# Column mean of an 8192 x 8192 matrix: which rows of the matrix each SBUF partition loads

## The chip, the cores and the metric

The kernel runs on one core of a Trainium2 chip. The metric is device time in microseconds (us) of one execution; the median of three runs of the kernel before is 627.79 us (627.75 to 627.97).

## The reference

The input `x` is a float32 matrix of 8192 x 8192, 256 MiB. The output is the mean of each column, 8192 numbers:

```python
def reference(x: np.ndarray) -> np.ndarray:
    return np.mean(x, axis=0)
```

Every input byte is needed once, and one addition is made per element.

## The kernel before, in words

Rows lie in memory one after the other, 32 KB each. A *slab* is 128 rows, one for each of the 128 SBUF partitions; there are 64 slabs. The first 62 are loaded as 31 *pairs*: a pair is 256 successive rows, 8 MB, and partition p takes rows 2p and 2p + 1 of the pair, which are 64 KB in one stretch. The helper `rows` (lines 58 to 60) forms this source. Three buffers `pairs[0..2]` of 128 x 16384 float32 are used in turn.

All loads are issued by SyncE, in order, on one DMA queue. `load` (line 77) issues the load of a pair, at line 83. Most loads take a whole pair. The first is cut after 2048 columns (`FIRST`), and the last three are cut between the two rows (`BY_ROW`). From pair 3 on, SyncE waits before a load until VectorE has added up the pair that the buffer held before (line 95, semaphore `read`). One load is carried out by sixteen DMA engines, each of which serves eight partitions.

VectorE does nearly all the adding, all at line 53. For each pair it waits until the data has landed (`take`, line 56, in the loop of line 99; by row at lines 105 and 107), adds the first rows to the running sum of the pair before, and then the second rows to that. Each of these is one instruction on 128 x 8192 elements. So one running sum per partition and column moves from buffer to buffer.

The last two slabs are loaded by themselves. The next to last, `slab`, comes in three loads (line 163), the last, `last`, in nine pieces of falling width (`PIECES`, line 166). TensorE sums over the partitions: it multiplies the running sum, the slab and the last slab by a matrix of ones, and accumulates in PSUM (`fold_wide` and `fold_narrow`, line 136), piece by piece as the last slab lands. VectorE adds the last quarter of `slab` itself. ScalarE and VectorE scale the totals by 1/8192 (lines 151 and 153), and SyncE stores them (lines 200 and 215).

The order of work on every engine is written out by hand, with semaphores; no planner rearranges it.

Of the kernel before, what the change touches and what calls it, by code (L numbers as in the profile page):

```python
# [21 lines left out]
def kernel(  # L22
# [5 lines left out]
    nc = tc.nc  # L28
    P = nc.NUM_PARTITIONS
    R, C = x.shape  # L30
    n_slabs = R // P
# [23 lines left out]
    def take(sem, n):  # L55
        nc.vector.wait_ge(sem, n).then_inc(sem, -n)  # L56

    def rows(k):
        src = x[2 * P * k : 2 * P * (k + 1), :]
        return src.rearrange("(p j) c -> p (j c)", j=2)  # L60

    def first_rows(b):
        ins = add(pairs[b][:, 0:C], pairs[b][:, 0:C], pairs[b - 1][:, 0:C])
# [13 lines left out]
    def load(k):  # L77
        b = k % 3
        cut = FIRST if k == 0 else C if k >= n_pairs - BY_ROW else 2 * C
        for lo, hi in ((0, cut), (cut, 2 * C)):  # L80
            if lo < hi:
                sem = second[b] if lo == C else landed[b]
                ins = nc.sync.dma_start(out=pairs[b][:, lo:hi], in_=rows(k)[:, lo:hi])
                yield ins.then_inc(sem, 16)
# [34 lines left out]
    def behind(ins, wait=False):  # L119
        kind = mybir.DependencyClass.Sync if wait else mybir.DependencyClass.NoSync  # L120
        info = mybir.DependencyInfo(kind, mybir.DependencyReason.DATA)
        tc.add_manual_dep(ins.ins, section.name, info, reason="the last pair's second rows")

    wide, lo = [], 0
# [31 lines left out]


    tail = pairs[n_pairs % 3]
    r = (n_slabs - 2) * P
    slab, last = tail[:, 0:C], tail[:, C : 2 * C]  # L160
    parts = [(lo, lo + w) for lo, w, _ in wide[:3]] + [(wide[3][0], C)]
    for lo, hi in ((0, C // 4), (C // 4, C // 2), (C // 2, C)):
        behind(nc.sync.dma_start(out=slab[:, lo:hi], in_=x[r : r + P, lo:hi]))  # L163
    lo = 0
    for w in PIECES:
        nc.sync.dma_start(out=last[:, lo : lo + w], in_=x[r + P : R, lo : lo + w])  # L166
        lo += w


# [3 lines left out]
    lo, hi = parts[3]  # L173
# [70 lines left out]
```

## Time and profile before

| | before |
|---|---|
| median of three runs | 627.79 us |
| profiled execution, its own time | 627.46 us |
| its span in the profile | 625.5 us |
| DMA engines, share of the span | 99.4% |
| read from HBM | 268.44 MB |
| mean rate over the span | 429 GB/s |
| VectorE busy | 533.6 us (85%) |
| one VectorE add, 128 x 8192 | 8.69 us |
| TensorE busy | 13.5 us (2%) |

The profile is of one execution. Its span goes from the first to the last instruction that the profiler records; the execution's own time is about 2 us longer. "Busy" is time in which an engine carries out an instruction of its own. For the DMA engines the share is the time that their packets took, in percent of sixteen engines' span. A wait is written as the engine and line that waited, an arrow, and what released it; a name like DVEq or SPq is the engine's own sequencer, in which a semaphore wait stands ahead of the work. DVE is VectorE, PE TensorE, ACT ScalarE, SP SyncE.

### The profile page before, as it was taken

Reading aid. Unit: us, or ns where it says so; the run is one execution under the profiler, and the core shown is the slowest. Engines: PE = TensorE matmul, PEld = TensorE weight load, DVE = VectorE, ACT = ScalarE, POOL = GpSimd, SP = SyncE. Lnnn points to the kernel's source line nnn. Section 1 sums busy time; section 2 is a strip of 40 time slices with the busy share of each in tenths; the row PEclk is TensorE's granted clock in tenths of the full one; section 3 lists DMA queues with packets and bytes.
Section 4 is the critical chain, followed back from the end, with each engine's and each line's share of the span. In section 5 each row is a group of like instructions: output and inputs, shape, how many; then the busy total and the mean of one; then the engine's idle time right before and its main releaser. Section 6 shows DMA issues by size and latency. Waiting matters only on the chain. (4 is left out here: it accounts for less than half of the span.)

```text
span 625.5 us, 520 instructions
## 1 busy us (share of the span) xinstructions
PE 13.5 (2%) x106; PEld 4.2 (1%) x106; DVE 533.6 (85%) x67; ACT 4.2 (1%) x7; POOL 0.3 (0%) x5
## 2 busy tenths in 40 slices
PE   0000000000000000000000000000000000000007
PEld 0000000000000000000000000000000000000002
DVE  0538988889888899888898888988889888899995
ACT  0000000000000000000000000000000000000001
POOL 0000000000000000000000000000000000000000
PEclk9999999999999999999999999999999999999999
DMA  9999999999999999999999999999999999999997
GB/s 404 400 469 402 469 402 469 402 469 402 469 402 465 407 423 448 402 469 402 469 402 469 402 469 402 469 402 469 402 461 411 440 432 419 423 432 436 436 429 312
DMA packets 6797, 268.49 MB, mean 429 GB/s; under 512 B 890, under 2 KB 1406, under 8 KB 1548
## 3 DMA queue, kind: packets, MB, share of 16 engines
q1 hardware_dynamic: 6796, 268.47, 99.4%
q8 instruction: 1, 0.02, 0.0%
HBM read 268.44 MB, written 0.03 MB: 429 GB/s over the span
## 5 line engine op out<-in xcount | busy, mean ns | idle before, releaser
L53 DVE TENSOR_TENSOR pair<-pair,pair 128x8192 f32<-128x8192 f32 (+1 forms) x31 | 263.1, 8486 | 60.9 <-DVEq L56 60.3
L53 DVE TENSOR_TENSOR pair<-pair 128x8192 f32<-128x8192 f32 (+1 forms) x34 | 269.7, 7938 | 23.8 <-DVEq L56 22.7
L136 PE MATMUL wide<-pair,ones 128*32 128x512 f32 (+1 forms) x88 | 12.0, 688 | 609.3 <-DVE pair L53 608.6
L136 PEld LDWEIGHTS wide<-pair,ones 128*32 128x32 f32 x88 | 3.2, 130 | 617.4 <-issue 614.1
L151 ACT ACT_TABLE_LOAD x1 | 1.3, 1283 | 602.9 <-ACTq L112 602.9
L153 DVE TENSOR_SCALAR row<-narrow 1x256 f32<-1x256 f32 x2 | 0.8, 415 | 4.8 <-PE narrow L136 4.8
L136 PE MATMUL narrow<-pair,ones 128*32 128x256 f32 (+2 forms) x18 | 2.0, 359 | 0.0
L151 ACT ACTIVATE rw<-wide 128x512 f32<-128x512 f32 x3 | 1.8, 597 | 15.6 <-PE wide L136 15.6
L136 PEld LDWEIGHTS narrow<-pair,ones 128*32 128x32 f32 x18 | 1.0, 109 | 0.9 <-DMA pair<-in_x_dram 0.5
L151 ACT ACTIVATE row<-narrow 1x256 f32<-1x256 f32 x2 | 0.8, 376 | 0.5 <-PE narrow L136 0.5
L151 ACT ACTIVATE r<-wide 128x256 f32<-128x256 f32 x1 | 0.4, 384 | 0.1
L92 POOL MEMSET ones<- 128x32 f32 x1 | 0.1, 124 | 0.3 <-POOLq L228 0.3
L228 POOL MEMSET const-bfloat16-1.0<- 128x1 bf16 x1 | 0.1, 101 | 0.0
L228 POOL MEMSET const-uint8-127<- 128x1 uint8 x1 | 0.1, 101 | 0.0
L228 POOL MEMSET const-float32-0.0<- 128x1 f32 x1 | 0.1, 98 | 0.2 <-issue 0.2
L228 POOL MEMSET const-float32-1.0<- 128x1 f32 x1 | 0.1, 98 | 0.0
## 6 DMA issues: line engine op xcount, KB each, us to landing
pair<-in_x_dram SPq DMA_DIRECT2D x6, 4096.0 KB, 25.5
pair<-in_x_dram SPq DMA_DIRECT2D x1, 7168.0 KB, 21.3
pair<-in_x_dram SPq DMA_DIRECT2D x6, 1024.0 KB, 8.7
pair<-in_x_dram SPq DMA_DIRECT2D x1, 2048.0 KB, 14.0
pair<-in_x_dram SPq DMA_DIRECT2D x1, 512.0 KB
pair<-in_x_dram SPq DMA_DIRECT2D x27, 29.7
pair<-in_x_dram SPq DMA_DIRECT2D x3, 128.0 KB, 15.5
pair<-in_x_dram SPq DMA_DIRECT2D x1, 80.0 KB, 9.9
```

Source lines behind the costliest of these rows:

```text
L53: return nc.vector.tensor_tensor(out=dst, in0=a, in1=b, op=ADD)
L92: tc.declare_fence(nc.gpsimd.memset(ones, 1.0).ins, group="ahead")
L136: nc.tensor.matmul(out=dst, lhsT=ones, rhs=src, skip_group_check=True, **flags)
L151: nc.scalar.mul(out=dst, in_=src, mul=inv_r)
L153: nc.vector.tensor_scalar(out=dst, in0=src, scalar1=inv_r, scalar2=None, op0=mybir.AluOpType.mult)
L228: nc = _bacc.Bacc("TRN2", target_bir_lowering=False, num_devices=1)
```

## The change

The 64 rows that a partition adds up are chosen differently. Partition p now holds rows 64p to 64p + 63. Load k takes from every partition's block its rows 2k and 2k + 1, again 64 KB in one stretch. The two last slabs are the rows 62 and 63 of every block. Between neighbouring partitions the source moves by 64 rows, 2 MB, in place of 64 KB (pairs) or 32 KB (slabs); between the first partitions of neighbouring DMA engines, by 16 MB in place of 512 KB. The mean is over all rows, so the result is the same up to the order of the additions.

```diff
+
+    by_part = x.rearrange("(p s) c -> p s c", s=n_slabs)
+
     def rows(k):
-        src = x[2 * P * k : 2 * P * (k + 1), :]
-        return src.rearrange("(p j) c -> p (j c)", j=2)
+        return by_part[:, 2 * k : 2 * k + 2, :].rearrange("p j c -> p (j c)")
...
     tail = pairs[n_pairs % 3]
-    r = (n_slabs - 2) * P
     slab, last = tail[:, 0:C], tail[:, C : 2 * C]
...
-        behind(nc.sync.dma_start(out=slab[:, lo:hi], in_=x[r : r + P, lo:hi]))
+        behind(nc.sync.dma_start(out=slab[:, lo:hi], in_=by_part[:, n_slabs - 2, lo:hi]))
     lo = 0
     for w in PIECES:
-        nc.sync.dma_start(out=last[:, lo : lo + w], in_=x[r + P : R, lo : lo + w])
+        nc.sync.dma_start(out=last[:, lo : lo + w], in_=by_part[:, n_slabs - 1, lo : lo + w])
         lo += w
```

## The prediction

> **What bounds the kernel now.** I read the page's busy shares first, then its DMA part, then a table of busy time and transfer rate by stretches, then the waits, and last the chain that set the end.
>
> ```profile
> span 625.5 us, 520 instructions
> PE 13.5 (2%) x106; PEld 4.2 (1%) x106; DVE 533.6 (85%) x67; ACT 4.2 (1%) x7; POOL 0.3 (0%) x5
> DMA packets 6797, 268.49 MB, mean 429 GB/s; under 512 B 890, under 2 KB 1406, under 8 KB 1548
> q1 hardware_dynamic: 6796, 268.47, 99.4%
> ```
>
> VectorE is busy for 85% of the span, but the sixteen DMA engines for 99.4%. They have no gap to fill: 99.4% of 625.5 us is 621.7 us, and all but a start of about 2 us and an end of about 2 us is transfer.
>
> The table by stretches gives busy time of each engine, granted clock, then the mean share of the DMA engines and their GB/s. Records are counted by whole transfers, so a share can read over 1; the quotient of the last two columns is the rate of a busy engine set.
>
> ```profile
> 0.00:2.00 2.00, 0.00 (x0) 0.00 (x0) 0.00 (x0) 0.00 (x0) 0.33 (x5) 1.00 0.33 49
> 3.00:4.00 1.00, 0.00 (x0) 0.00 (x0) 0.00 (x0) 0.00 (x0) 0.00 (x0) 1.00 1.02 434
> 20.00:120.00 100.00, 0.00 (x0) 0.00 (x0) 78.86 (x10) 0.00 (x0) 0.00 (x0) 1.00 1.00 431
> 120.00:220.00 100.00, 0.00 (x0) 0.00 (x0) 90.27 (x11) 0.00 (x0) 0.00 (x0) 1.00 1.00 432
> 320.00:420.00 100.00, 0.00 (x0) 0.00 (x0) 90.32 (x12) 0.00 (x0) 0.00 (x0) 1.00 0.99 430
> 420.00:520.00 100.00, 0.00 (x0) 0.00 (x0) 90.34 (x11) 0.00 (x0) 0.00 (x0) 1.00 1.02 440
> 610.00:615.00 5.00, 5.00 (x32) 1.39 (x28) 5.00 (x3) 0.00 (x0) 0.00 (x0) 1.00 0.98 416
> ```
>
> The quotient is 431, 432, 434 and 431 GB/s in the four long rows: it does not move. The single transfer records say the same more sharply: the 3,456 pieces of 64 KB (one piece is what one partition takes from one load) have a median of 2.418 us, the shortest is 2.415 and the longest 2.575; 65,536 bytes in 2.418 us on 16 engines is 433.7 GB/s. The 768 pieces of 32 KB all take 1.213 us. So today the engines run at a rate of their own and the memory never holds them up. Only the first row differs: 49 GB/s at a share of 0.33 is 148 GB/s while busy. Its sixteen first records, 8 KB each, took 0.68 to 1.16 us, 0.86 in the mean, where later pieces of 8 KB take 0.309.
>
> ```profile
> DVE pair L53 <- DVEq L56: 49.6, 26, 2.0
> SPq L83 <- DVEq L69: 557.8, 28, 48.0
> DMA 3%; PE 1%; SPq 0%; ACT 0%; issue 0%
> ```
>
> The first line is the waits between 60 and 560 us: before each pair of rows VectorE waits about 1.9 us for data. A pair needs 2 x 8.69 = 17.4 us of adding and 8 x 2.418 = 19.3 us of loading. The second line, SyncE waiting for VectorE to free a buffer, looks large and costs nothing: it waits with two loads queued ahead. The chain that ended last is made of the last slab's loads, then some 5 us of matmul, scaling and store. The kernel is its load stream: 620 us of data at 433 GB/s, and 7.5 us around it up to the profiled execution's own 627.46 us (its span is 625.5). That is 0.33 us, 0.05%, under the median of 627.79, so the sum below stands for either.
>
> **The change, part by part.** *Instructions.* The diff touches source addresses only. Loads, SyncE's issues (328 ns each at line 83), waits, adds, matmuls and stores stay in number and order: 0 us, and nothing is queued behind anything new. *Pieces.* Each load still takes 64 KB in one stretch per partition (8 to 56 KB where it is cut), and the row sums take part in a mean over all rows, so any distribution of rows serves. Per engine: 27 loads x 8 partitions = 216 pieces of 64 KB, 8 of 56 KB and 8 of 8 KB from load 0, 6 x 8 = 48 of 32 KB from the loads cut by row, 24 from the slab and 72 from the last slab: 376, of which 272 are of 32 KB or more. Same counts after: 0 us.
>
> *Places.* This is the only cost. Before, a pair is one block of 8 MB, and engines at 8 partitions each stand 512 KB apart; afterwards partitions are 64 x 32 KB = 2 MB apart and engines 16 MB. Whether the memory serves sixteen streams at such distances at 433 GB/s is not in the trace. From below: a gain can only come out of what the engines now lose to memory. That is 0.55 us at the first records and (2.4197 mean - 2.418) x 216 = 0.4 us, about 1 us together. From above: the row in which memory sets the time is the start, where a piece pays 0.86 - 0.31 = 0.55 us more; on all 376 pieces of an engine that is 207 us, so 835 us.
>
> Between 0 and 207 us I take a loss. For none speak two rows: the slab's pieces, whose partitions lie only 32 KB apart in place of 64, run at the same rate (its 16 KB pieces take 0.611 us, a quarter of 2.418 and 0.006), so halving a distance did nothing; and an engine's step from one load to the next, which jumps past the other engines' blocks, leaves no piece longer than 2.575 us. But both were seen at distances up to 8 MB inside one block, and all sixteen engines together covered every address of that block. After the change sixteen streams that are equally far have all address digits below 2 MB in common; a memory whose parts are chosen by these digits serves them by turns. The nearest row for an engine that waits for memory is the start, and of it I take the smallest extra, 0.68 - 0.31 = 0.37 us, since some of a first access comes once only. I charge it to the pieces of 32 KB or more: at the start the second piece of an engine took 0.31 to 0.46 us, so small pieces overlap each other. 272 x 0.37 = 101 us; 627.5 + 101 = 728.5 us, say **729**. A 64 KB piece then takes 2.79 us, the stream runs at 376 GB/s, and a pair takes 22.3 us. Nothing covers this, since the DMA engines have no idle time. VectorE is no bound at either rate; its wait grows from 1.9 to about 4.9 us per pair and takes nothing off.
>
> A rule speaks against the change. The Trainium skill, on the page "DMA: Bandwidth & Descriptors", section "Latency and other measured facts", reports copies between tensors in HBM with one row per partition: 207 GB/s in each direction at a pitch of 512 KiB, 164 at 2 MiB and 103 at 4 MiB, restored by a padding of 4 KiB. By the ratio 164/207 the 620 us become 783 and the kernel 790 us, an estimate from that page. No run here shows a pitch of 2 MB yet; the copies write to HBM too, which this stream doesn't.
>
> **The rivals.** *Nothing changes, 627.5 us (chance 0.23).* The memory has room for sixteen streams wherever they are. For it: the constant 2.418 us, the unmoved slab. Against it: both come from close places. It decides if 64 KB pieces stay at 2.42 us.
>
> *Full contention, around 835 us (0.24, from 765 up).* The streams meet at one part of memory throughout, and every piece, small ones too, pays what the first ones paid: 376 x 0.55 = 207 us. For it: engines with like addresses have nothing to drive them apart except their own delays. Against it: those delays do drive them apart, and a stream that has fallen behind by one part of memory no longer collides. It takes the place of the forecast from 0.5 us extra per large piece (136 us). About a third of it lies beyond 835. I give it as much as no change, since the rows show both what a first access costs and that close places cost nothing, and none lies at 2 MB. The Trainium skill's rule above, 790 us, would fall in this case; no trace so far bears on that.
>
> *A small loss, 629 to 663 us (0.09).* The pieces stretch no more than the longest seen: 2.575 - 2.418 = 0.157 us on 216 + 8 pieces is 35 us. That is what memory refusals already look like mid-run, rarely.
>
> *Faster (0.04).* The place is the start and the few stretched pieces: if the engines, far apart, no longer hinder one another there, the 1 us above is won, 626.5 us. It would have to be more than 1.26 us, 0.2%, to decide, and the rows hold no more; the chance stands for what they can't show. A faster stream in the middle is excluded as far as the rows reach: a piece that never varies isn't waiting for memory.
>
> **How the numbers follow.** The forecast, a sustained loss of 0.13 to 0.5 us per large piece, has a chance of 0.40, and its own range is 663 to 765 us. With 0.24, 0.23, 0.09 and 0.04 for the others that makes 1. Slower by over 0.2% (about 1.26 us, what a measurement of this kernel can tell from no change): 0.40 + 0.24 + 0.09 = 0.73. Within: 0.23. Faster: 0.04. The range must hold both no change and most of full contention, so it goes from 626.5 (the lower edge of no change) to 835; outside lie the faster case, 0.04, and some 0.08 above.
>
> **What would show it.** In the DMA part the share should stay near 99% while the mean falls from 429 to about 370 GB/s, with the same 6,800 packets. The 64 KB records should have a median near 2.8 us and a spread, where now there is none; the wait at line 56 should rise to about 5 us per pair; the adds should stay at 8.69 us. If the pieces stay at 2.42 us, the step from addresses to contention is wrong. If they stretch to 3 us or more, my price per piece was too low; if only the tail from 598 us on grows, it is the small pieces that pay, against my choice. Different packet counts would mean that the loads were cut otherwise, which I hold excluded.

## The result and the profile after

The change makes the kernel slower: median 663.83 us of eight runs (653.85 to 670.3) against 627.77 (627.43 to 627.97). The ratio is 1.0435, 95% interval 1.0421 to 1.045; it rests on the three shortest of the eight runs, because the other five, the profiled one among them, lie over 1.5% above the shortest, and the kernel before shows no such scatter. Two later sets of four gave 1.0559 (1.0516 to 1.0602) and 1.03 (1.0283 to 1.0317) on two different chips. So the medians of the sets lie 19 to 36 us above the kernel before, and the loss is not a fixed number. I had forecast 101.

The profiled execution after took 664.72 us. These lines of its page are the span, the GB/s in 40 equal slices, the packets and the load queue's share:

```profile
span 662.8 us, 520 instructions
GB/s 285 364 396 415 431 407 427 443 411 411 415 407 439 423 407 439 439 423 419 431 439 411 415 439 407 419 443 427 435 423 423 439 443 415 392 425 415 363 278 115
DMA packets 6797, 268.49 MB, mean 405 GB/s; under 512 B 890, under 2 KB 1406, under 8 KB 1548
q1 hardware_dynamic: 6796, 268.47, 98.3%
```

Instructions and packets are the same as before, and the DMA engines are still busy all the time. They do the same work at 405 instead of 429 GB/s. The slices show where: at 285 and 364 in the first two, 278 and 115 in the last two, and in between a little under the old rate. The table by stretches (columns as in the prediction: clock, DMA share and GB/s at the end of each line) says the same for the changed kernel in absolute time:

```profile
0.00:20.00 20.00, 0.00 (x0) 0.00 (x0) 0.00 (x0) 0.00 (x0) 0.33 (x5) 1.00 0.86 282
20.00:40.00 20.00, 0.00 (x0) 0.00 (x0) 8.69 (x1) 0.00 (x0) 0.00 (x0) 1.00 1.03 396
100.00:200.00 100.00, 0.00 (x0) 0.00 (x0) 86.91 (x11) 0.00 (x0) 0.00 (x0) 1.00 1.00 418
400.00:600.00 200.00, 0.00 (x0) 0.00 (x0) 180.32 (x21) 0.00 (x0) 0.00 (x0) 1.00 0.99 423
640.00:650.00 10.00, 1.93 (x8) 0.20 (x8) 2.29 (x1) 0.41 (x1) 0.00 (x0) 0.65 1.00 230
650.00:655.00 5.00, 2.65 (x16) 0.68 (x20) 0.00 (x0) 0.79 (x2) 0.00 (x0) 0.50 0.74 187
```

In the first row the engines are busy for 0.86 of the time and move 282 GB/s, 328 while busy: they are held up, and not only idle. At 20 to 40 us it is 385, later 418 to 427. From 640 to 650 us the engines are fully busy at 230 GB/s. The kernel before moved this in the same first stretch:

```profile
0.00:20.00 20.00, 0.00 (x0) 0.00 (x0) 0.00 (x0) 0.00 (x0) 0.33 (x5) 1.00 0.99 414
```

The transfer records give the price by size. Mean time of a piece (what one partition takes from one load) in us, and how many pieces an engine carries:

| piece | per engine | before | after | extra per engine |
|---|---|---|---|---|
| 64 KB | 216 | 2.420 | 2.477 | 12.3 |
| 56 KB (first load) | 8 | 2.117 | 2.620 | 4.0 |
| 32 KB | 48 | 1.213 | 1.288 | 3.6 |
| 16 KB | 8 | 0.611 | 0.796 | 1.5 |
| 8 KB | 48 | 0.322 | 0.469 | 7.1 |
| 4 KB | 8 | 0.159 | 0.312 | 1.2 |

The last column, count times difference, sums to 29.7 us. Relative to its length a 64 KB piece pays 2%, a 4 KB piece 96%. The median of the 64 KB pieces is unchanged at 2.418 us: most pay nothing, and one in five took over 2.5 us, 2.70 in the mean and up to 3.58. The price is highest at the start but does not end there: of the 19.9 us that the pieces of 32 KB or more pay per engine, 7.7 fall to pieces that start in the first 100 us, 8.6 between 100 and 560, and 3.6 later.

The chains that ended last put the rest in place. In the kernel before the chain has 18.03 us of loads and then 24 wide matmuls of 2.35 us in all, which start at 617.21 us, 8.3 us before the end of the span:

```profile
599.13 18.03 DMA pair<-in_x_dram
617.16 0.04 issue
617.21 2.35 PE wide L136 x24
```

After:

```profile
620.77 31.54 DMA pair<-in_x_dram
652.31 0.04 issue
652.35 4.47 PE wide L138 x24
656.82 0.43 PE narrow L138 x8
```

Here the 24 matmuls start at 652.35, 10.5 us before the end. So 35.1 us of the 37.3 by which the span grew are loads, of which 29.7 are the pieces' own time. The remaining 5 are time in which engines had no piece: the share fell from 0.99 to 0.86 in the first 20 us, and it is 0.74 at 650 to 655 us; how the 5 us divide was not worked out. The other 2.2 us are mostly TensorE: the same 24 matmuls took 4.47 in place of 2.35 us, at a granted clock of 0.50 in that stretch.

VectorE's wait before each pair, between 60 and 590 us, is now about 2.4 us in place of 1.9; its adds are unchanged (533.5 us in all). In the line below the longest wait, 13.7 us, belongs to the add that runs from 51.72 to 60.41 us, so it lies before the stretch: (74.9 - 13.7) / 26 = 2.4.

```profile
DVE pair L53 <- DVEq L56: 74.9, 27, 13.7
```

### The profile page after: what moved, and what is told of

Its sections match the earlier page's. It is cut to its first block, busy times and chain, and to the rows that moved or that the text cites. A ratio compares the mean times of both kernels' runs of the same rounds, so it can differ in the third digit from the quotient of the medians.

```text
span 662.8 us, 520 instructions
## 1 busy us (share of the span) xinstructions
PE 16.2 (2%) x106; PEld 4.1 (1%) x106; DVE 533.5 (80%) x67; ACT 4.1 (1%) x7; POOL 0.3 (0%) x5
## 2 busy tenths in 40 slices
DMA packets 6797, 268.49 MB, mean 405 GB/s; under 512 B 890, under 2 KB 1406, under 8 KB 1548
## 5 line engine op out<-in xcount | busy, mean ns | idle before, releaser
L53 DVE TENSOR_TENSOR pair<-pair,pair 128x8192 f32<-128x8192 f32 (+1 forms) x31 | 263.1, 8486 | 81.1 <-DVEq L56 74.9
L138 PE MATMUL wide<-pair,ones 128*32 128x512 f32 (+1 forms) x88 | 15.2, 836 | 643.1 <-DVE pair L53 630.5
```

Source lines behind the costliest of these rows:

```text
L53: return nc.vector.tensor_tensor(out=dst, in0=a, in1=b, op=ADD)
L138: nc.tensor.matmul(out=dst, lhsT=ones, rhs=src, skip_group_check=True, **flags)
```

## The experiments

**Theory A**: the sixteen engines' streams, a multiple of 2 MB apart, agree in all address digits below 2 MB as long as they are equally far; then they hold each other up. Delays drive them apart, and the loss ends, until small pieces or a new start bring them together again. **B**, my prediction's price: each piece of 32 KB or more pays, always; small ones don't. **C**: the distance itself costs, since each piece opens a far place. Distances between engines are counted here, as in the prediction, as though each engine served eight neighbouring partitions; no run shows which partitions an engine serves. What each variant sets for certain is the distance between partitions.

### One part alone: the pairs, or the last two slabs

The pairs after the change, the slabs as before:

```diff
-        behind(nc.sync.dma_start(out=slab[:, lo:hi], in_=by_part[:, n_slabs - 2, lo:hi]))
+        behind(nc.sync.dma_start(out=slab[:, lo:hi], in_=x[r : r + P, lo:hi]))
...
-        nc.sync.dma_start(out=last[:, lo : lo + w], in_=by_part[:, n_slabs - 1, lo : lo + w])
+        nc.sync.dma_start(out=last[:, lo : lo + w], in_=x[r + P : R, lo : lo + w])
```

(`r` is the first row of the last two slabs, as before the change.)

> Only the 31 pairs are read in blocks 2 MB apart; the last two slabs are read as before, rows 7936 to 8191 (so rows 62 and 63 of each block are left out and the last 256 rows count twice). Theory A (streams that agree in their address digits below 2 MB collide, worst where pieces are small): the large pieces of the changed kernel's profile lost 12.4 + 4.0 + 3.6 us per engine and the first small ones 1 to 2, so 646 to 651 us. Theory B (my prediction's price: only pieces of 32 KB or more pay, small ones overlap): the whole loss stays, 654 us or more.

Measured: 637.83 us, ratio 1.0176 (1.0151 to 1.0201), a loss of 10 us. That is less than either theory said. Its stretches:

```profile
0.00:20.00 20.00, 0.00 (x0) 0.00 (x0) 0.00 (x0) 0.00 (x0) 0.33 (x5) 1.00 0.94 313
20.00:40.00 20.00, 0.00 (x0) 0.00 (x0) 8.69 (x1) 0.00 (x0) 0.00 (x0) 1.00 1.01 401
40.00:60.00 20.00, 0.00 (x0) 0.00 (x0) 10.31 (x2) 0.00 (x0) 0.00 (x0) 1.00 0.98 413
60.00:100.00 40.00, 0.00 (x0) 0.00 (x0) 34.93 (x5) 0.00 (x0) 0.00 (x0) 1.00 1.00 429
100.00:200.00 100.00, 0.00 (x0) 0.00 (x0) 89.86 (x11) 0.00 (x0) 0.00 (x0) 1.00 1.00 433
200.00:400.00 200.00, 0.00 (x0) 0.00 (x0) 178.71 (x22) 0.00 (x0) 0.00 (x0) 1.00 1.00 434
```

The rate climbs from 313 to 433 GB/s within the first 100 us and stays there, with the partitions still 2 MB apart. The 64 KB pieces that start in the first 40 us of loading have a mean of 2.65 us, in the next 40 of 2.47, then 2.44, and after 120 us 2.42. A price per piece (B) or per distance (C) cannot end like that.

The slabs after the change, the pairs as before (the opposite edit):

> Only the last two slabs are read with partitions 2 MB apart (rows 62 and 63 of each block, so some rows count twice and others are left out); the pairs as before. Theory A: the small pieces of a slab all lie in one window of 1 to 16 KB below 2 MB, so they collide more than large ones: 8 to 16 us over the kernel before, 636 to 644 us. Theory B: small pieces pay nothing, 627 to 629 us.

Measured: 636.35 us, ratio 1.0139 (1.0122 to 1.0156), a loss of 8.6 us where B had none: small pieces do pay. Their issues, with KB each and median us from issue to landing:

```profile
pair<-in_x_dram SPq DMA_DIRECT2D x3, 128.0 KB, 23.4
pair<-in_x_dram SPq DMA_DIRECT2D x1, 80.0 KB, 16.4
pair<-in_x_dram SPq DMA_DIRECT2D x1, 48.0 KB, 12.9
```

In the kernel before:

```profile
pair<-in_x_dram SPq DMA_DIRECT2D x3, 128.0 KB, 15.5
pair<-in_x_dram SPq DMA_DIRECT2D x1, 80.0 KB, 9.9
pair<-in_x_dram SPq DMA_DIRECT2D x1, 48.0 KB, 7.7
```

The 4 KB pieces took 0.424 us in place of 0.159, those of 8 KB 0.420 in place of 0.322, those of 16 KB 0.696 in place of 0.611.

### The engines put in step again

From the fourth load on, each load is issued only when no other is in flight, in both layouts:

```diff
         for k in range(3, n_pairs):
-            nc.sync.wait_ge(read, k - 2)
+            nc.sync.wait_ge(read, k - 1)
```

> The kernel before, but from the fourth load on each load is issued only when VectorE has added up the pair before it, so that no two of these loads are in flight together and all sixteen engines start each load in the same moment. The control: about 31 x (19.3 + 17.4 + 2) = 1200 us, pieces of 64 KB at 2.42 us as ever, whatever the theory.

> The same restraint on the changed kernel. Theory A with drift (the loss is that of engines in step; delays drive them apart within the first 80 us or so, and then large pieces run free): each load puts them in step again, so the 64 KB pieces stay at the 2.6 to 2.75 us of the first loads all through, some 0.25 us x 216 = 55 us and the tail over the control. Rival (a loss that comes with time or once at the start, say a first touch of far places): pieces of 64 KB at 2.42 to 2.45 us after the first loads, and 10 to 30 us over the control.

Measured: 932.74 us and 1076.41 us, one run each. The control came out well below my 1200: 932.74 / 31 is 30.1 us per pair, which fits one load of 19.3 us, one add of 8.69 and some 2 us. So the signal comes once the first of the two adds is done: in the control's timeline a load is issued at 316.91 us, 0.06 us after a pair's second add has begun. The difference of 143.7 us is 2.6 times the 55 us that I expected before the tail. Issue to landing of a whole load in the control:

```profile
pair<-in_x_dram SPq DMA_DIRECT2D x27, 21.8
```

and with the change:

```profile
pair<-in_x_dram SPq DMA_DIRECT2D x27, 26.2
```

The 64 KB pieces have a median of 2.872 us against 2.420 in the control, and the median does not fall with time: between 2.74 and 2.96 in every stretch of 40 us. The control's mean is 2.497, above its median, because of the restart itself: in the whole loads that are issued one at a time, the first sixteen pieces of a load take 3.09 us in the mean and all later ones 2.42. With the change the first sixteen take 3.58, and the later ones 2.79 to 2.99, without a fall from the second sixteen to the eighth. So with every load started afresh the streams lose 0.45 us per large piece by the medians, and this neither ends within a load of some 25 us nor wears off over the run; in the pairs-only kernel above, where loads follow each other without a gap, it wore off in some 100 us. That the engines are in step is inferred from this; the trace does not say which engine carried a piece. A rival by which far places cost at their first touch alone falls here.

### Smaller pieces in the middle of the run

The 27 whole loads cut into four of half a row each; VectorE waits for all four:

```diff
+        q = C // 2
+        spans = [(a, a + q) for a in range(0, 2 * C, q)] if cut == 2 * C else ((0, cut), (cut, 2 * C))
-        for lo, hi in ((0, cut), (cut, 2 * C)):
+        for lo, hi in spans:
...
-                take(landed[b], 16)
+                take(landed[b], 64)
```

> The kernel before with the 27 whole loads cut into four of 16 KB per partition (half a row each). The control: 4 x 0.611 = 2.444 us for 64 KB in place of 2.418, so 633 to 636 us whatever the theory.

> The same cut on the changed kernel: the bytes and places are the same, but the 128 pieces of one load lie in a window of 16 KB below 2 MB in place of 64 KB, so engines that drifted apart within a load meet again. Theory A: pieces of 16 KB at the 0.70 to 0.80 us that they take in the tails read 2 MB apart, so 864 x 0.09 to 0.19 us = 75 to 160 us over the control. Rival (only the start and the smallest pieces collide): 10 to 30 us over the control.

Measured: 630.87 and 716.96 us, one run each. The old layout bears the cut almost for nothing, 2 us less than I expected; between the layouts there are now 86.1 us in place of 19 to 36. The same stretch of the control:

```profile
200.00:400.00 200.00, 0.00 (x0) 0.00 (x0) 179.04 (x21) 0.00 (x0) 0.00 (x0) 1.00 1.01 431
```

and with the change:

```profile
200.00:400.00 200.00, 0.00 (x0) 0.00 (x0) 156.85 (x19) 0.00 (x0) 0.00 (x0) 1.00 1.00 380
```

Now the rate never recovers: 382, 380 and 390 GB/s in the stretches from 100 to 600 us. The 16 KB pieces took 0.679 us in the mean against 0.611. All 128 pieces of such a load lie within 16 KB below 2 MB, so by theory A engines that had come apart meet again. The same reading would explain why the tail pays most, byte for byte; the 1 MB variant below speaks against it as a general rule.

### The pitch: distance or digits

The change's layout with other distances between partitions; the source is written out as an access pattern, for the last two slabs' loads as well:

```diff
+    pitch = 64 * C - 1024
+
+    def part(at, n):
+        return bass.AP(tensor=x.tensor, offset=x.offset + at, ap=[[pitch, P], [1, n]])
...
     def rows(k):
-        return by_part[:, 2 * k : 2 * k + 2, :].rearrange("p j c -> p (j c)")
+        return part(2 * k * C, 2 * C)
```

`pitch` counts elements of 4 bytes; the other variants have 63 * C, 32 * C, 16 * C and 64 * C - 48.

> All loads as after the change, but partitions 2 MB less 4 KB apart (pieces then start inside rows, so the output is not the column mean). Engines still stand 16 MB less 32 KB apart. Theory A: the shared digits are gone, 627 to 630 us. Theory C (distance itself costs, each piece opens a far place): as the change, 654 to 670 us.

> All loads as after the change, but partitions 63 rows apart, 2 MB less 32 KB (rows at block ends count twice, the last 64 rows are left out in part). Engines stand 16 MB less 256 KB apart. Theory A: 627 to 630 us. Theory C: 654 to 670 us.

> All loads as after the change, but partitions 1 MB (32 rows) apart, engines 8 MB (blocks overlap, so half of the rows are read twice and the others left out). Theory A, if every power of two from 1 MB up shares one part of the memory: 645 to 670 us as the change. If one more address digit tells the engines apart: 630 to 645 us. Theory C (distance): no less than half the loss, 640 us or more.

> Partitions 512 KB (16 rows) apart, engines 4 MB (rows are read up to four times, most left out). Theory A with address digits that tell engines apart: 627 to 632 us. If all powers of two collide alike: 645 to 670 us.

> All loads as after the change, but partitions 2 MB less 192 bytes apart (pieces start inside rows, so the output is not the column mean); engines 16 MB less 1.5 KB apart, the whole fan of sixteen within 24 KB below 2 MB. If a shift of a few KB from engine to engine is enough: 630 to 635 us, near the 4 KB variant's 630.9. If the shift must move engines by tens of KB: 650 to 670 us as the change.

| distance of partitions | distance over eight partitions | median us | ratio (95% interval) |
|---|---|---|---|
| 2 MB (the change, three sets) | 16 MB | 646.43 to 663.83 | 1.03 to 1.0559 |
| 2 MB less 192 B | 16 MB less 1.5 KB | 637.74 | 1.0157 (1.014 to 1.0174) |
| 2 MB less 4 KB | 16 MB less 32 KB | 630.93 | 1.0047 (1.003 to 1.0064) |
| 2 MB less 32 KB | 16 MB less 256 KB | 627.30 | 0.9995 (0.9986 to 1.0005) |
| 1 MB | 8 MB | 644.45 | 1.0258 (1.0223 to 1.0293) |
| 512 KB | 4 MB | 627.73 | 1.0001 (0.9991 to 1.001) |

The variants ran on three chips, and on each of them the whole change or one of its parts lost 8.5 us or more. Theory C is out: at nearly the same distance, 32 KB less, nothing is lost. With 4 KB less, 630.93 us is just outside theory A's 627 to 630. The 192-byte variant fell between its two expectations. It ran beside the change on one chip (646.43) and took 8.7 us of its 18.6 us off: its 64 KB pieces were at a mean of 2.42 us from the start, while its 8 KB pieces still took 0.414 us.

Two results theory A does not explain as it stands. Partitions 512 KB apart agree in their low address digits too, and over eight partitions in all digits below 4 MB, yet nothing is lost; so agreement below 2 MB is not enough, and what tells the streams apart there stays open. And with partitions 1 MB apart, on the chip on which the whole change took 662.97, the large pieces lose and the tail does not. Its 64 KB pieces have a mean of 2.472 us, its 4 KB pieces took 0.159 us as before the change, and its small loads land as they did then:

```profile
pair<-in_x_dram SPq DMA_DIRECT2D x3, 128.0 KB, 15.6
pair<-in_x_dram SPq DMA_DIRECT2D x1, 80.0 KB, 9.9
pair<-in_x_dram SPq DMA_DIRECT2D x1, 48.0 KB, 7.8
```

So small pieces in one narrow window of addresses need not collide: they did at 2 MB and did not at 1 MB.

The Trainium skill's row that the prediction cited ("DMA: Bandwidth & Descriptors", "Latency and other measured facts") has the same order: nearly full rate at 512 KiB, less at 2 MiB, and a padding of 4 KiB at a pitch of 4 MiB restores it. These runs agree on that order, at a smaller size: 3 to 5.6% more time, where its copies fell from 207 to 164 GB/s. So the 790 us that the prediction estimated by that ratio did not come. The Trainium skill found 192 bytes of padding to be no help at 4 MiB; here 2 MB less 192 bytes took about half of the loss off.

### A column mean in blocks, without the collision

Partition p takes rows 62p to 62p + 61, and the last 256 rows are the two slabs, read as before. This computes the same mean:

```diff
-    by_part = x.rearrange("(p s) c -> p s c", s=n_slabs)
+    by_part = x[0 : (n_slabs - 2) * P, :].rearrange("(p s) c -> p s c", s=n_slabs - 2)
```

and with the slab loads of `main_only`.

> Partition p holds rows 62p to 62p + 61, and the last two slabs are the last 256 rows, read as before: the column mean over all rows. Partitions stand 62 rows, 2 MB less 64 KB, apart, engines 15.5 MB. Theory A (shared address digits): as the kernel before, 627 to 629 us. Theory C (distance): as main_only, 636 to 641 us.

Measured: 627.24 us, ratio 0.9994 (0.9985 to 1.0003). It differs from the pairs-only kernel in nothing but the block's 62 rows for 64, and the loss is gone. The pairs-only kernel took 637.83 and 639.84 us on two other chips; on this chip the whole change took 662.97. Nor is it faster than the kernel before.

```profile
span 625.2 us, 520 instructions
DMA packets 6797, 268.49 MB, mean 429 GB/s; under 512 B 890, under 2 KB 1406, under 8 KB 1548
```

### Do the parts add up?

Pairs alone cost 10 us and slabs alone 8.6, but the whole change 27 and more. Those sets ran on different chips. The changed kernel was run again:

> The changed kernel, beside the next three on one chip, since its loss (27 us and more) is larger than main_only's 10 and tail_only's 8.6 together. If the parts only add up and the rest is chance of the execution: 645 to 650 us here. If main and tail work on each other, or the streams settle differently each time: 653 to 670 us again.

Measured: 662.97 us, no nearer to the sum. Its profile repeats the first one: 64 KB pieces with a mean of 2.474 us, and 420 to 429 GB/s in the stretches from 100 to 600 us. Then the whole and its two parts, side by side on one chip:

> The changed kernel, on one chip with its two parts. If the parts add up there: main_same_chip + tail_same_chip - 628, within 3 us. If they work on each other: 8 us or more above that sum.

> Pairs in blocks 2 MB apart, last slabs as before (rows 62 and 63 of each block left out, the last 256 rows twice). If how the streams settle belongs to the chip and the execution: 645 to 655 us here when the whole change takes 660. If it belongs to this kernel: 636 to 641 us as at first.

> Pairs as before, last slabs with partitions 2 MB apart (some rows twice, others left out). The small pieces all lie in one window: 635 to 638 us as at first, on any chip.

Measured: 646.43, 639.84 and 636.26 us against 627.79. On that chip the parts cost 12.1 and 8.5 us, which sums to 648.3; the whole is 1.9 us below it. They add up there. What varies is mainly how the pairs' stream settles: pieces of 32 KB or more pay 7.2 us per engine in this profile and 19.9 and 19.0 in the two others, pieces of 4 to 16 KB 8.5, 9.8 and 10.9. On that chip the changed kernel ran at 433 GB/s from 100 us on:

```profile
100.00:200.00 100.00, 0.00 (x0) 0.00 (x0) 89.72 (x11) 0.00 (x0) 0.00 (x0) 1.00 1.00 433
200.00:400.00 200.00, 0.00 (x0) 0.00 (x0) 178.96 (x21) 0.00 (x0) 0.00 (x0) 1.00 1.00 433
```

while the profile of the first set stayed at 418 to 426 through those stretches: there the streams met again and again, without a new start that the profile shows. Whether the chip, the place of the matrix in memory or something else makes the difference stays open.

## Why the prediction was wrong

**The bound** was read rightly. DMA engines busy for 99.4%, a VectorE with 1.9 us to spare per pair: a slower stream goes into the time whole, and 35.1 of the 37.3 us of growth were loads.

**Instructions and pieces at 0 us**: right. 520 instructions, 6,797 packets and the same busy time of VectorE.

**The sign and the kind of cause**: right. The streams hold each other up because of where the partitions lie, since 62 or 63 rows per block in place of 64 lose nothing. The step that "sixteen streams that are equally far have all address digits below 2 MB in common" is not the whole of it: over eight partitions that holds at 512 KB as well, where nothing was lost. The distances of 512 KB and 16 MB between engines are a count by eight neighbouring partitions that no run shows. The rival of no change (0.23) fell.

**The step that failed** is the sum 272 x 0.37 = 101 us: the term of the large pieces was mis-sized. By the table above these 272 pieces paid 12.3 + 4.0 + 3.6 = 19.9 us, 0.07 us each. The price of one collision was about right: the 64 KB pieces over 2.5 us paid 0.28 us in the mean, and with each load started afresh a piece pays 0.45. (The records of the start give 0.67 us for the shortest first piece and 0.88 for the mean, where the prediction read 0.68 and 0.86; that moves the 101 by 3 us only.) Wrong was to charge it to every large piece: one 64 KB piece in five took over 2.5 us. Left to run on, the streams come apart; in the pairs-only profile the price fell from 0.24 us to nothing within some 120 us. In the changed kernel's own profile it fell too but came back, with 8.6 of the 19.9 us between 100 and 560 us, and why it came back there and not on the chip of the last set (0.6 us there) is open. The prediction had the reason in hand: under full contention it says that the delays drive the streams apart and that "a stream that has fallen behind by one part of memory no longer collides". It used this against the dearer rival alone, when it held against the forecast as well.

**"Small pieces overlap each other", so 0 us for them**: wrong. The first load's small pieces were one row from a cold start. Pieces of 4 to 16 KB paid 1.5 + 7.1 + 1.2 = 9.8 us per engine, nearly all of it in the tail; the slabs alone cost 8.6 us of the kernel's time. I had named the growth of the tail as the sign against this choice, and it showed.

**The cases.** What came is the case that I gave 0.09, "a small loss, 629 to 663 us", with the first set's median of 663.83 just past its upper edge, where the forecast's own range begins. The range of 626.5 to 835 holds it; the forecast of 729 was 65 us too long. Full contention (0.24) was right that small pieces pay, but most pieces paid nothing. The price of the small loss, 0.157 us on all large pieces, came from the longest piece of the kernel before and was no better reasoned than the other; it was nearer because it was small. Signs that I had named: the mean of 370 GB/s (405 measured), pieces at a median of 2.8 us (2.418), a wait of 5 us per pair (2.4) all failed the same way.

## What to carry to other kernels

Before choosing a layout that gives each partition a long block of a matrix, work out the distance between the partitions' places: 1 MB and 2 MB cost time here and 512 KB did not, and a few rows less per block (62 for 64) cost nothing. Where streams hold each other up, do not charge the price of one collision to every transfer; ask what lets them come apart: free-running large transfers lost 0.07 us each, the same transfers started together, load by load, lost 0.45. And look at the small transfers of the tail by themselves: at 2 MB they paid most for their length.

## What the runs showed of the hardware that I had not expected

- Colliding load streams can order themselves. With the pairs' loads at partitions 2 MB apart (pairs alone) the rate rose from 313 to 433 GB/s in 100 us without any instruction to that end. In two profiles of the whole change it stayed at 418 to 429 between 100 and 600 us.
- Partitions 1 MB apart slowed the large pieces and not the small ones (64 KB in 2.472 us in place of 2.420, 4 KB in 0.159 as before); partitions 2 MB apart slowed both (2.477 and 0.312 us).
- The size of the loss varies for the same program: 646 us on one chip and 663 on another, while the kernel before stayed at 627.2 to 628.1 in every set.
- Late loads went with a slower TensorE. In the changed kernel it sat idle for 9.64 us up to 647.6 us, waiting for a load; its granted clock was 0.65 at 640 to 650 us and 0.50 at 650 to 655, and 24 matmuls took 4.47 us, where the kernel before had a clock of 1.00 in its tail and took 2.35. These 2 us of the end were in no step of mine; that the idle time lowered the clock was not tried by itself.
